# A tiny ScalarE write ahead of the second tile's load, in a two-tile row normalisation

## The chip, the cores and the metric

The kernel runs on one core of a Trainium2 chip. The metric is the device time of one execution in microseconds, lower is better. Executions of one kernel here agree within about 0.6% (81.74 to 82.21 us in 34 runs of the kernel before), so effects of 0.3% are read from means over several runs, with a 95% interval. A run counts as slow when it is over 1.5% above the fastest run of its kernel. All runs that carry the argument are fast; the one kernel for which that is not so is marked. The granted clock is 1.0 in every run.

## The reference

```
norm = sqrt(sum(x ** 2, axis=-1, keepdims=True) + eps)     # x: 1024 x 4096 float32
return x / norm
```

Each of 1024 rows is divided by its own norm. 16.78 MB come in and 16.78 MB go out.

## The kernel before

The 1024 rows are two tiles of 128 partitions x 4 rows of 4096. Each tile has its own buffer, one load and one store of 8.4 MB, so nothing waits for a buffer. SyncE issues all four transfers on one queue. ScalarE squares and sums rows 0 to 2, VectorE row 3; ScalarE takes the roots, VectorE the reciprocals and nearly all scaling. In this cut (left-out lines are `...`, the comments are added) `R` is 4 rows and `D` is 4096.

```python
# class RowGroups: square_act, square_dve, norm (ScalarE root, VectorE reciprocal), scale (VectorE)
def scale_by_both(self, r):
    cut = 7 * self.D // 8        # ScalarE scales [:cut], VectorE the rest
    ...
groups = []
for i in range(n_tiles):
    g = RowGroups(nc, io, stats, scratch, D, R, eps_t)
    load = nc.sync.dma_start(out=g.flat(), in_=x_t[i])
    if i == 0:
        first_load_to_front(nc, load.ins)     # ahead of the opening barrier
    groups.append(g)
for i, g in enumerate(groups):
    g.square_dve(R - 1)
    g.square_act(0)
    g.norm(0)
    g.scale(0)
    g.square_act(1)
    g.norm(1)
    g.norm(R - 1)
    g.scale(1)
    g.scale(R - 1)
    g.square_act(2)
    g.norm(2)
    if i < n_tiles - 1:
        g.scale_by_both(2)
    else:
        g.scale(2)
    store = nc.sync.dma_start(out=out_t[i], in_=g.flat())
...
```

The build orders the instructions of each engine itself, within their dependences. The order of the source is not always the order that runs: in the first tile of this kernel, the build takes the root of row 3 (`g.norm(R - 1)`) ahead of the square of row 1. This matters below.

## Time and profile before

| | before |
|---|---|
| median time of 3 runs | 81.92 us (81.88 to 81.94) |
| span of the profile | 80.1 us |
| DMA queue, share of 16 engines | 97.3% |
| VectorE, ScalarE busy | 33%, 37% |
| issues of load 1, load 2, store 1, store 2 | 0.00, 0.79, 38.83, 56.62 us |

How to read it: the DMA engines work almost without a break, so the compute engines matter only through the moments at which they let a transfer be issued. The lines are shown in the prediction.

### The profile page before, as it was taken

To read this page: it belongs to the slowest core of one execution; us is meant where nothing else is said; L and a number is where in the kernel's file an instruction comes from. 1 tells how busy PE (TensorE), PEld (TensorE's weight loads), DVE (VectorE), ACT (ScalarE), POOL (GpSimd) and SP (SyncE) were. 2 spreads that over 40 slices of the span, in tenths; PEclk is the share of its full clock that TensorE was granted. 3 is DMA by queue.
4 is the path that set the end of the run, shared out by engine and by line. 5 is a ranking of instruction groups with operands and counts; after the bars stand their busy time and mean duration, and the time that the engine had idled before them with its cause. 6 is when DMAs were issued, how large, how long until landed. Compare 5 with 4: busy or idle time off the path is not lost.

```text
span 80.1 us, 93 instructions
## 1 busy us (share of the span) xinstructions
DVE 26.7 (33%) x21; ACT 29.7 (37%) x23; POOL 0.2 (0%) x4
## 2 busy tenths in 40 slices
DVE  0000000000099599960039995999200000000000
ACT  6000000000099999989339999950000000000000
POOL 0000000000000000000000000000000000000000
DMA  9199996599993899993999993999993999993990
GB/s 491 65 491 524 524 524 295 229 524 524 524 524 164 360 524 524 524 491 164 393 524 524 524 458 164 425 524 524 524 425 164 458 524 524 524 425 131 491 524 0
DMA packets 576, 33.55 MB, mean 419 GB/s; under 512 B 64, under 2 KB 64, under 8 KB 64
## 3 DMA queue, kind: packets, MB, share of 16 engines
q1 hardware_dynamic: 576, 33.55, 97.3%
HBM read 16.78 MB, written 16.78 MB: 419 GB/s over the span
## 4 chain that ended last, share of the span: by engine, by line
DMA 50%; ACT 10%; DVE 9%; issue 0%
DMA xt<-in_x_dram 50%; ACT sq_act L33 9%; DVE xt L64 9%; ACT rstd L53 1%; DVE rstd L59 0%
## 5 line engine op out<-in xcount | busy, mean ns | idle before, releaser
L33 ACT ACTIVATE sq_act<-xt 128x4096 f32<-128x4096 f32 x6 | 21.7, 3608 | 22.3 <-DMA xt<-in_x_dram 22.3
L42 DVE SCALAR_TENSOR_TENSOR sq_dve<-xt 128x4096 f32<-128x4096 f32 x2 | 8.9, 4426 | 26.3 <-DMA xt<-in_x_dram 26.3
L64 DVE TENSOR_SCALAR xt<-xt,rstd 128x4096 f32<-128x4096 f32 x7 | 16.5, 2354 | 0.2
L72 ACT ACTIVATE xt<-xt,rstd 128x3584 f32<-128x3584 f32 x1 | 3.3, 3282 | 0.2 <-DVE rstd L59 0.2
L53 ACT ACTIVATE rstd<-ssq,eps_t 128x1 f32<-128x1 f32 x8 | 2.1, 288 | 0.1
L59 DVE RECIPROCAL rstd<-rstd 128x1 f32<-128x1 f32 x8 | 1.3, 160 | 2.4 <-ACT rstd L53 2.4
L33 ACT ACT_TABLE_LOAD x1 | 1.3, 1283 | 0.8 <-PEq L256 0.8
L53 ACT ACT_TABLE_LOAD x1 | 1.3, 1283 | 0.0
L33 ACT ACTIVATION_READ_ACCUMULATOR sq_act<-xt 128x1 f32 x6 | 1.1, 186 | 0.0
L78 DVE TENSOR_SCALAR xt<-xt,rstd 128x512 f32<-128x512 f32 x1 | 0.5, 486 | 0.0
L209 DVE MEMSET eps_t<- 128x1 f32 x1 | 0.1, 59 | 0.9 <-PEq L256 0.9
L42 DVE DVE_READ_ACCUMULATOR sq_dve<-xt 128x1 f32 x2 | 0.2, 83 | 0.0
L256 POOL MEMSET const-bfloat16-1.0<- 128x1 bf16 x1 | 0.1, 102 | 0.0
L256 POOL MEMSET const-uint8-127<- 128x1 uint8 x1 | 0.1, 101 | 0.0
L256 POOL MEMSET const-float32-0.0<- 128x1 f32 x1 | 0.1, 99 | 0.2 <-issue 0.2
L256 POOL MEMSET const-float32-1.0<- 128x1 f32 x1 | 0.1, 98 | 0.0
## 6 DMA issues: line engine op xcount, KB each, us to landing
xt<-in_x_dram SPq DMA_DIRECT2D x2, 31.2
out_dram<-xt SPq DMA_DIRECT2D x2, 22.5
```

The costliest lines, as they stand in the source:

```text
L33: self.nc.scalar.activation(out=sq_a, in_=self.x[:, r], func=ACT_F.Square, accum_out=self.ssq[:, r : r + 1],)
L42: self.nc.vector.scalar_tensor_tensor(out=sq_v, in0=self.x[:, r], scalar=1.0, in1=self.x[:, r], op0=ALU.mult, op1=ALU.mult, accum_out=self ...
L53: self.nc.scalar.activation(out=self.rstd[:, r : r + n], in_=self.ssq[:, r : r + n], func=ACT_F.Sqrt, bias=self.eps_t,)
L59: self.nc.vector.reciprocal(out=self.rstd[:, r : r + n], in_=self.rstd[:, r : r + n])
L64: self.nc.vector.tensor_scalar_mul(out=self.x[:, r], in0=self.x[:, r], scalar1=self.rstd[:, r : r + 1])
L72: self.nc.scalar.activation(out=self.x[:, r, :cut], in_=self.x[:, r, :cut], func=ACT_F.Copy, scale=rstd,)
L78: self.nc.vector.tensor_scalar_mul(out=self.x[:, r, cut:], in0=self.x[:, r, cut:], scalar1=rstd)
L209: nc.vector.memset(eps_t, eps)
L256: nc = _bacc.Bacc("TRN2", target_bir_lowering=False, num_devices=1)
```

## The change

The second tile's first column gets a tiny write by ScalarE, so the second load, which overwrites it, must wait for that write. The evident intent is to keep the second load out of the way while the first one starts.

```diff
         g = RowGroups(nc, io, stats, scratch, D, R, eps_t)
+        if i == 1:
+
+            nc.scalar.activation(out=g.x[:, 0, 0:1], in_=eps_t, func=ACT_F.Square)
         load = nc.sync.dma_start(out=g.flat(), in_=x_t[i])
```

## The prediction

> **What bounds the kernel now.** I began with the page's busy shares and its DMA row, then the DMA queue, then the timeline around each transfer, then narrow windows at the start, because the rest turned out to have no room.
>
> ```profile
> DVE 26.7 (33%) x21; ACT 29.7 (37%) x23; POOL 0.2 (0%) x4
> DMA  9199996599993899993999993999993999993990
> ...
> q1 hardware_dynamic: 576, 33.55, 97.3%
> HBM read 16.78 MB, written 16.78 MB: 419 GB/s over the span
> ```
>
> The compute engines are busy a third of the span; the 16 DMA engines are busy 97.3% of it. So the kernel is bound by moving 33.55 MB, and 2.7% of 80.1 us, 2.2 us, is all the time in which they are not. The dips in the DMA row are no idle time: the program has four transfers (two loads, two stores) of 128 rows of 64 KB, thus 512 large packets, 32 for each engine, and a packet seems to be counted where it starts, so a slice in which few start looks empty. Two windows settle the length of one:
>
> ```profile
> core 0: us, DVE busy (x) ACT busy (x) POOL busy (x), PEclk, DMA share, GB/s
> 0.00:1.00 1.00, 0.06 (x1) 0.21 (x1) 0.20 (x4) 1.00 0.00 0
> 1.00:1.25 0.25, 0.00 (x0) 0.25 (x1) 0.00 (x0) 1.00 5.64 1835
> 1.25:1.50 0.25, 0.00 (x0) 0.25 (x1) 0.00 (x0) 1.00 2.89 1049
> 1.50:1.75 0.25, 0.00 (x0) 0.25 (x1) 0.00 (x0) 1.00 1.39 524
> 1.75:2.00 0.25, 0.00 (x0) 0.25 (x1) 0.00 (x0) 1.00 1.29 524
> 2.00:2.25 0.25, 0.00 (x0) 0.07 (x1) 0.00 (x0) 1.00 0.64 262
> ...
> 3.90:4.75 0.85, 0.00 (x0) 0.00 (x0) 0.00 (x0) 1.00 2.85 1234
> ...
> 37.75:38.50 0.75, 0.00 (x0) 0.75 (x1) 0.00 (x0) 1.00 3.24 1398
> ```
>
> The last two columns are the DMA share and the rate; the rate times the window's length, over 65,536 bytes, counts the packets that start in it. In 3.90:4.75 that is 1234 x 0.85 us = 1.05 MB = 16 packets, one for each engine, and 2.85 x 0.85 x 16 / 16 = 2.42 us each. At that length 32 packets take 77.4 us. In the first rows 7, 4, 2, 2 and 1 packets start, so the sixteen engines do not begin together: the first starts just after 1.0 us, the last just after 2.0 us. The first seven take 5.64 x 0.25 x 16 / 7 = 3.22 us each, the next four 2.89, then about 2.8 and 2.6. After that all is regular. The end follows: last engine starts at 2.0, plus 77.4, gives 79.4; its slow first packet and the landing account for the rest of the 80.1 us span. **The only slack is the first two microseconds**: a wait of 1.0 us before any packet, a stagger of 1.0 us, and a first packet that is up to 0.8 us too long.
>
> Next, whether compute ever holds up the DMA:
>
> ```profile
> 0.00 1.12 SPq L217 DMA_DIRECT2D xt<-in_x_dram  x2
> ...
> 0.79 1.28 ACT L33 ACT_TABLE_LOAD   x1 [0.79 <-PEq L256]
> 0.86 0.06 DVE L209 MEMSET eps_t<- 128x1 f32 x1 [0.86 <-PEq L256]
> ...
> 38.83 0.35 SPq L238 DMA_DIRECT2D out_dram<-xt  x1
> 41.26 3.62 ACT L33 ACTIVATE sq_act<-xt 128x4096 f32<-128x4096 f32 x1 [2.45 <-DMA xt<-in_x_dram]
> ...
> 56.62 0.34 SPq L238 DMA_DIRECT2D out_dram<-xt  x1
> ```
>
> The first store is issued at 38.83, while the second load lands at about 41.2: it queues 2.4 us ahead of need. The second store is issued at 56.62. The first store, begun when the load was done, lasts a quarter of 77.4 us, 19.4 us, to about 60.6: 4 us ahead of need. Both exceed the 1.0 us that an issue needs before its first packet (seen at the start). So the queue never runs dry, and nothing that ScalarE or VectorE does shows in the end time. The chain of waits charges "DMA xt<-in_x_dram 50%" from 0.79 us, the issue of the second load; that is the time it stands behind the first one in the queue, and starting it later need not move its landing.
>
> **What the Trainium skill says.** "DMA: Bandwidth & Descriptors", section "Queues, rings and completion order": on each DMA engine descriptors are consumed in ring order. The trace agrees: both loads are on q1 and land about 19.3 us apart (21.94 and 41.26), so the second does not share the rate with the first. The same page, "Where 436 GB/s comes from", gives a ceiling of 435.2 GB/s for the ports. Here 16 x 65,536 B / 2.42 us = 433 GB/s, so between packets there is nothing to win. "Perfetto Trace Analysis", its part on the HWDGE DMA instruction, says that the profiled span of an issue covers the generation of descriptors and not the movement. The trace agrees: an issue shows about 0.35 us, yet no packet starts before 1.0 us. "ScalarE: Activation LUTs", section "What ACT_TABLE_LOAD costs", gives 1283 ns for the load and 280 ns + 0.833 ns per element for an ACTIVATE with a pointer bias; the rows here have 1283 ns and 288 ns for 128x1.
>
> **The change part by part.** It adds one ACTIVATE of 128x1 on ScalarE before the second load is issued, and as that write goes to the same tile, the load must wait for it. Nothing is removed.
> - Its own cost: about 0.29 us (from the 128x1 Sqrt row) on an engine that would sit idle until 21.94. On the path: 0. It reads eps_t, ready at 0.92, and uses Square, the function whose table is loaded first anyway, so I expect no third table load.
> - The wait: the table load ends at 0.79 + 1.28 = 2.07; plus 0.29 is 2.36. The second load is issued at about 2.4 instead of 0.79, 1.6 us later. Its first packet is needed when the first load's eight packets per engine are done, at about 20.9 us at the earliest. With 1.0 us from issue to first packet it is ready at 3.4, some 17 us early. Cost on the path: 0.
> - What moves: the generation of the second load's descriptors leaves the stretch in which the first load's packets begin. It now falls between 0.79 and, by the 1.0 to 2.0 us that the first load's own took to reach its engines, some 1.8 to 2.8 us. That covers the late half of the stagger and the long first packets. This must be the intent: let the first load start undisturbed. At most it is worth the stagger plus a bit: if all engines started near 1.0 with packets of 2.42 us, the end would come at 1.0 + 77.4 plus the same tail, 1.0 to 1.2 us earlier. But a transfer needs some time to reach sixteen engines whatever follows it, and a first packet also waits for its first bytes, so I give the second load less than half of it: 0.4 us. Against that stands the same disturbance at its new place, 2.4 to 4.4 us. The first store's issue at 38.83 shows its size in full flow: packets started in 37.75:38.50 last 3.24 x 0.75 x 16 / 16 = 2.43 us instead of 2.42, thus 0.01 us. Hence about -0.4 us in all: 81.92 to 81.5.
>
> **The rivals.**
> 1. No overlap matters: the stagger and the long first packets belong to the first load itself (cold memory, its own descriptors). For it: the earliest engines, started at 1.0 to 1.2, are the slow ones, which looks like a wait common to all that ends at about 2 us, rather than a queue behind the second load. Then the time is 81.9.
> 2. A real gain at the start, the whole stagger: 80.8 to 81.0. For it: the first load has the stretch to itself until 2.4. Against it: the second load's issue begins only 0.2 us before the first packets.
> 3. The wait moves trouble into the first packets, still running until 4.6 us: the descriptors arrive at 3.4 to 4.4, and if they slow packets as much as the start seems to, the gain is given back, or up to 0.3 us lost: 82.2. Against it: the 0.01 us at the first store.
> 4. The delay uncovers the second load, or a table is loaded thrice and the first store is late. The margins are 17 us and 2.4 - 1.0 = 1.4 us against 1.6 us and 1.28 us; the second margin is close, but the first tile's table reload at 25.7 exists already. I give this 1%.
>
> **Range and chances.** The limits are the slack at the start on one side, 1.2 us, and the small disturbance on the other. I predict 81.5 us and a range of 80.8 to 82.1. Two per cent is 1.64 us, more than the whole stagger and the long first packets together can give; only if the 1.0 us wait before the first packet also shrank would it be reached, and that wait begins before the second load is issued. So: faster by over 2% 0.02, within 2% 0.96, slower by over 2% 0.02.
>
> **What would show it.** In the trace after, one more 128x1 ACTIVATE at about 2.1 us, the second load's issue near 2.4, still two table loads, and both landings moved by the same small amount as the end. The windows from 1.0 to 2.25 should have more packets early and a mean nearer to 2.42 us; if their counts stay 7, 4, 2, 2, 1 with the same means, rival 1 holds. If the windows around 3.9 to 4.75 show packets well over 2.42 us, rival 3 does. The prediction is wrong in kind if the gap between the two landings exceeds 19.4 us, or if the issue of the first store comes after the second load has landed.

## The result, and the profile after

The kernel after takes 82.28 us (median of 6 runs, 82.2 to 82.43) against 81.93 us of the kernel before in the same session (6 runs). The ratio is 1.0041, 95% interval 1.0028 to 1.0054. Ratios here are the mean time of one kernel's fast runs over that of the other's of the same rounds, so not quite the ratio of the medians quoted. The change makes the kernel slower by 0.35 us. It is within 2%, as predicted (in part by luck, see below), but outside the range of 80.8 to 82.1, and in the opposite direction to the gain that was predicted.

The tiny write and the wait came out as worked out. From the timeline of the kernel after (start, duration, engine, line, operation):

```profile
0.79 1.28 ACT L219 ACT_TABLE_LOAD   x1 [0.79 <-PEq L259]
2.09 0.20 ACT L219 ACTIVATE xt<-eps_t 128x1 f32<-128x1 f32 x1
2.31 0.33 SPq L220 DMA_DIRECT2D xt<-in_x_dram  x1
```

The start did not get faster. These are the windows of the kernel after at the start; the last two columns are DMA share and GB/s, read as in the prediction:

```profile
1.00:1.25 0.25, 0.00 (x0) 0.25 (x1) 0.00 (x0) 1.00 7.16 2359
1.25:1.50 0.25, 0.00 (x0) 0.25 (x1) 0.00 (x0) 1.00 2.20 786
1.50:1.75 0.25, 0.00 (x0) 0.25 (x1) 0.00 (x0) 1.00 0.00 0
1.75:2.00 0.25, 0.00 (x0) 0.25 (x1) 0.00 (x0) 1.00 1.84 786
2.00:2.25 0.25, 0.00 (x0) 0.24 (x2) 0.00 (x0) 1.00 0.61 262
...
3.90:5.00 1.10, 0.00 (x0) 0.00 (x0) 0.00 (x0) 1.00 2.20 953
```

Now 9, 3, 0, 3 and 1 packets start, instead of 7, 4, 2, 2 and 1. Summed up, the sixteen first packets take 0.25 x 16 x (7.16 + 2.20 + 1.84 + 0.61) / 16 = 2.95 us on average; the same sum over the prediction's rows gives 2.96 us. The first load starts just as slowly with the second one out of the way. The second packets, in 3.90:5.00, last 2.20 x 1.10 x 16 / 16 = 2.42 us as before, so the wait did no harm there either (rival 3). Both loads also land as before (the second tile's work starts at 41.29 instead of 41.26).

The loss is at the border between the last load and the first store. First the kernel before, then the kernel after, same windows. The first row of each block has the starts of the load's last packets, the next two have what follows them, and the last is near the end of the program:

```profile
37.80:38.50 0.70, 0.00 (x0) 0.70 (x1) 0.00 (x0) 1.00 3.47 1498
...
40.24:40.52 0.28, 0.00 (x0) 0.00 (x0) 0.00 (x0) 1.00 2.71 1170
40.52:40.92 0.40, 0.00 (x0) 0.00 (x0) 0.00 (x0) 1.00 4.17 1802
...
77.12:77.48 0.36, 0.00 (x0) 0.00 (x0) 0.00 (x0) 1.00 0.00 0
```

```profile
37.80:38.50 0.70, 0.00 (x0) 0.70 (x1) 0.00 (x0) 1.00 3.46 1498
...
40.24:40.52 0.28, 0.00 (x0) 0.00 (x0) 0.00 (x0) 1.00 0.01 0
40.52:40.92 0.40, 0.00 (x0) 0.00 (x0) 0.00 (x0) 1.00 5.01 2130
...
77.12:77.48 0.36, 0.00 (x0) 0.00 (x0) 0.00 (x0) 1.00 4.21 1820
```

In both kernels all sixteen engines start their last load packet between 37.80 and 38.50. In the kernel before, 1170 GB/s x 0.28 us / 65,536 B = 5 engines go on to a store packet between 40.24 and 40.52. In the kernel after none does: the first store packet starts at 40.53. By the records of the single packets, an engine now idles 0.21 us on average here, against 0.002 us before. At the end, 10 engines start their last packet after 77.12 that had all started it by then in the kernel before.

The cause is one step earlier. This is VectorE and ScalarE on the first tile, before and after:

```profile
26.96 0.48 ACT L53 ACTIVATE rstd<-ssq,eps_t 128x1 f32<-128x1 f32 x2
27.29 0.16 DVE L59 RECIPROCAL rstd<-rstd 128x1 f32<-128x1 f32 x1 [0.92 <-ACT rstd L53]
27.35 3.60 ACT L33 ACTIVATE sq_act<-xt 128x4096 f32<-128x4096 f32 x1
...
35.33 0.17 DVE L59 RECIPROCAL rstd<-rstd 128x1 f32<-128x1 f32 x1 [0.56 <-ACT rstd L53]
```

```profile
26.98 0.29 ACT L53 ACTIVATE rstd<-ssq,eps_t 128x1 f32<-128x1 f32 x1
27.18 3.60 ACT L33 ACTIVATE sq_act<-xt 128x4096 f32<-128x4096 f32 x1
...
30.78 0.46 ACT L53 ACTIVATE rstd<-ssq,eps_t 128x1 f32<-128x1 f32 x2
31.09 0.16 DVE L59 RECIPROCAL rstd<-rstd 128x1 f32<-128x1 f32 x1 [1.23 <-ACT rstd L53]
...
36.02 0.15 DVE L59 RECIPROCAL rstd<-rstd 128x1 f32<-128x1 f32 x1
...
39.52 0.35 SPq L241 DMA_DIRECT2D out_dram<-xt  x1
```

Before, ScalarE takes two roots (rows 3 and 0) at 26.96, ahead of its next big square, so VectorE has two rows to scale while that square runs. After, it takes only the root of row 0, then squares row 1 for 3.6 us, and only then takes the roots of rows 3 and 1. VectorE idles 1.23 us up to 31.09, works the rest off in a row, and comes to the last reciprocal at 36.02 instead of 35.33. The first store is issued at 39.52 instead of 38.83, 0.69 us later. The diff says nothing of this order: the build chose it. The late order is the order of the source; the early one was the build's own doing, and with the added write it did not do so.

### The profile page after: what moved, and what is told of

Same layout as the page of the kernel before. It is cut to its first block, busy times and chain, and to the rows that moved or that the text cites. A ratio compares the mean times of both kernels' runs of the same rounds, so it can differ in the third digit from the quotient of the medians.

```text
span 80.5 us, 94 instructions
## 1 busy us (share of the span) xinstructions
DVE 26.7 (33%) x21; ACT 29.8 (37%) x24; POOL 0.2 (0%) x4
## 4 chain that ended last, share of the span: by engine, by line
DMA 48%; ACT 12%; DVE 9%; issue 0%
DMA xt<-in_x_dram 48%; ACT sq_act L33 9%; DVE xt L64 9%; ACT L219 2%; ACT rstd L53 1%; DVE rstd L59 0%; ACT xt L219 0%
```

## The experiments

Twelve experiments ran, on eleven kernels (the last is a second look at one); all gave correct results. The edits are shown shortened, with lines joined. The first four take the change apart.

**late_order.** The kernel before, with an ordering edge (a dependence given to the build) and nothing else; the arguments of the edge and two `return` lines are left out here:

```diff
+        sq1 = g.square_act(1)
         g.norm(1)
-        g.norm(R - 1)
+        root = g.norm(R - 1)
+        if i == 0:
+            # edge without semaphore: root after sq1 on ScalarE
```

> The kernel before, with nothing but ScalarE's order in the first tile forced to that of the kernel after (the square root of row 3 after the square of row 1). No tiny write, no wait. Theory A (the order makes the first store late): first store issued near 39.5 us, its first packets about 1.0 us later at 40.5 instead of 40.24, time 82.2 to 82.35. Theory B (the wait of the second load costs): unchanged, 81.9.

Measured: 82.26 us, ratio 1.0033 (1.0022 to 1.0045). The first store was issued at 39.49. Its windows:

```profile
40.18:40.41 0.23, 0.00 (x0) 0.00 (x0) 0.00 (x0) 1.00 0.01 0
40.41:40.86 0.45, 0.00 (x0) 0.00 (x0) 0.00 (x0) 1.00 4.79 2039
```

No store packet starts before 40.41, though the first engine's load packets were done at 40.19. The order alone, with no write and no wait, brings the whole loss.

**early_order.** The kernel after, with the opposite edge: in the first tile the root of row 3 is taken before the square of row 1. The tiny write and the wait stay.

> The kernel after with its tiny write and its wait, but ScalarE's order in the first tile forced back to that of the kernel before. Theory A: second load issued near 2.3 us, first store near 38.8 us, no gap before the store's packets, time 81.85 to 82.0. Theory B (the wait or the write costs by itself): stays at 82.2 to 82.35.

Measured: 81.93 us, ratio 0.9997 (0.9988 to 1.0006). Second load issued at 2.30, first store at 38.78. The same windows:

```profile
40.18:40.41 0.23, 0.00 (x0) 0.00 (x0) 0.00 (x0) 1.00 2.64 1140
40.41:40.86 0.45, 0.00 (x0) 0.00 (x0) 0.00 (x0) 1.00 4.04 1748
```

4 and 12 packets start, without a pause. So the tiny write and the wait together cost nothing and gain nothing that shows.

**op_alone.** The tiny write goes to a scratch column; the second load waits for nothing.

```diff
-            nc.scalar.activation(out=g.x[:, 0, 0:1], in_=eps_t, func=ACT_F.Square)
+            nc.scalar.activation(out=stats.tile([P, 1], F32, name="tiny"), in_=eps_t, func=ACT_F.Square)
```

> The tiny Square writes to a scratch column, so that the second load waits for nothing. The build gives ScalarE the order of the kernel after. Theory A: second load issued near 0.8 us again, first store still near 39.5 us, time 82.2 to 82.35. Theory B (the wait): 81.9. My theory at the prediction (the late second load helps the start a little): 82.5, as that help would be gone.

Measured: 82.27 us, ratio 1.0038 (1.0025 to 1.0051). Second load at 0.78, first store at 39.51. The mere presence of the instruction makes the build choose the later order. My reason at the prediction, that a late second load helps the start, missed: with the load early again nothing was lost.

**wait_dve.** The write is a memset on VectorE, so there is a wait but no ScalarE instruction (shown against the kernel after).

```diff
-            nc.scalar.activation(out=g.x[:, 0, 0:1], in_=eps_t, func=ACT_F.Square)
+            nc.vector.memset(g.x[:, 0, 0:1], 0.0)
```

> The tiny write is a memset on VectorE instead, so the second load waits, but only to about 1.0 us, and the build keeps ScalarE's order of the kernel before. Theory A: first store near 38.8 us, time 81.85 to 82.0. Theory B (any wait for a write): 82.1 or more.

Measured: 81.89 us, ratio 0.9998 (0.9988 to 1.0007); second load at 0.97, first store at 38.70, and the build kept the earlier order. These four leave one cause: the order. That it acts through the late store is tested next.

The next ones ask how late is too late, and what it costs.

**after_cut58.** The kernel after, `cut = 5 * self.D // 8` in place of `7 * self.D // 8`, so that ScalarE's share of the last scaling ends sooner.

> The kernel after as it is (tiny write, wait and ScalarE's late order), but the last scaling of the first tile cut at 5/8 instead of 7/8, so that ScalarE's part takes about 3.28 - 1024 x 0.833 ns = 2.43 us. Theory A (only the moment of the first store counts, it must be issued by 40.24 - 1.01 = 39.2 us): store issued near 38.7 us, no gap, time 81.85 to 82.0. If the order or the tiny write costs in any other way, it stays near 82.25.

Measured: 81.97 us, ratio 1.000 (0.999 to 1.001), first store at 38.63, no gap. Order, write and wait are those of the kernel after; a store 0.89 us earlier is enough to undo the loss. So the order costs only through the moment of the first store.

**before_cut63.** The kernel before with `cut = 63 * self.D // 64`.

> The kernel before with the last scaling of the first tile cut at 63/64, so that ScalarE's part takes 448 x 0.833 ns = 0.37 us longer. The first store should be issued near 39.2 us, at the limit. Theory A with its limit of 39.2: gap of 0.0 to 0.05 us, time 81.9 to 82.05. If any delay of the store costs from the start (a slope without a limit): 82.25 or so.

Measured: 82.09 us, ratio 1.002 (1.0012 to 1.0029), first store at 39.15. The time is just outside what I expected, as my limit of 39.2 was wrong. Call the time from the issue to the moment when an engine is done with the load that engine's lead. The engines were done from 40.16 to 40.84. By the records of the single packets, three of them, with leads of 1.45, 1.59 and 1.69 us, went straight on to a store packet of 2.42 us; the other thirteen, with leads of 1.01 to 1.51 us, idled 0.21 us on average (0.17 us over all sixteen). In the kernel before, issued at 38.83, the smallest lead was 1.41 us (first engine done at 40.24) and no engine idled; in the kernel after the largest was 1.40 us and all did. So a store's issue must come about 1.4 to 1.5 us before an engine runs out, not 1.0 us, and the limit is not a sharp one.

**late_cut63.** The forced late order plus the cut at 63/64.

> The forced late order on the kernel before, plus the cut at 63/64: first store near 39.86 us. Theory A: the gap grows by the same 0.37 us, from 0.2 to about 0.57 us, time 82.26 + 0.37 = 82.6 to 82.7. If the loss of late_order was a fixed price of missing the limit: 82.26 again.

Measured: 82.18 us, ratio 1.0033 (1.0021 to 1.0045), first store at 39.77. The expectation missed: 0.28 us more delay than in late_order, and the mean gap went only from 0.20 to 0.23 us. So it is not a gap that grows with the delay from the limit on; the price looks fixed.

**late_split.** As late_cut63, with ScalarE's last scaling in four pieces. This separates a fixed price from one that grows later.

```diff
-        self.nc.scalar.activation(out=self.x[:, r, :cut], in_=self.x[:, r, :cut], func=ACT_F.Copy, scale=rstd)
+        for a in range(0, cut, cut // 4):
+            self.nc.scalar.activation(out=self.x[:, r, a : a + cut // 4],
+                in_=self.x[:, r, a : a + cut // 4], func=ACT_F.Copy, scale=rstd)
```

> Late order, cut at 63/64, and ScalarE's last scaling of the first tile made in four pieces, for some 0.5 us more: first store near 40.3 us. Theory C (an engine pays a fixed 0.2 us when its next descriptors are late, and beyond that only waits until they are there, 0.86 us after the issue in late_cut63): first store packets at about 40.3 + 0.86 = 41.2 us, mean gap 0.6 to 0.9 us, time 82.6 to 82.9. Theory D (one fixed price however late): 82.2 to 82.3 again.

Measured: 82.72 us, ratio 1.0096 (1.0082 to 1.0111), first store at 40.52. Its windows:

```profile
40.90:41.36 0.46, 0.03 (x1) 0.03 (x1) 0.00 (x0) 1.00 0.00 0
41.36:41.52 0.16, 0.16 (x1) 0.16 (x1) 0.00 (x0) 1.00 15.36 6554
```

All sixteen engines start at once after 41.36, 0.84 us after the issue, with a mean gap of 0.78 us. This is what theory C had. So for this store there are two regimes. An engine for which the issue comes too late, by the limit of about 1.4 us, but still well ahead pays about 0.2 us; one with a lead of less than about 0.6 us is idle until 0.84 to 0.99 us after the issue (late_split; the least in late_cut63 is 0.86). What the engine does in the 0.2 us is not shown.

The last four test the other margin of the prediction, that of the second load, by making it wait for a row of big VectorE writes to its tile (shown against the kernel after):

```diff
-            nc.scalar.activation(out=g.x[:, 0, 0:1], in_=eps_t, func=ACT_F.Square)
+            nc.vector.memset(g.x[:, 0], 1.0)
+            for k in range(5):      # wait_edge: 6; wait_gap: 6 and half a row more
+                nc.vector.tensor_scalar_mul(out=g.x[:, (k + 1) % 2], in0=g.x[:, k % 2], scalar1=1.0)
```

**wait_long.**

> The second load waits for six big VectorE writes to its tile, five of them of 2.35 us, and is issued only at about 15 to 17 us, 13 us later than in the kernel after; ScalarE's order is that of the kernel before. Theory A (the load needs its descriptors only at about 20.9 us, so it may be issued as late as 19.9): no gap, first store near 38.8 us, time 81.85 to 82.05. Theory B (a late second load costs): clearly over 82.3.

Measured: 81.89 us, ratio 1.0002 (0.9993 to 1.001). The load was issued at 16.87 and cost nothing.

**wait_edge.**

> As wait_gap, but without the last half write: the second load is issued near 19.2 us, some 1.7 us before the first engine runs out of packets (20.9). In before_cut63 engines with a lead of 1.0 to 1.5 us ran dry and the one with 1.7 did not. Theory C: no gap between the loads, or at a few engines only, time 81.85 to 82.1. If the long row of VectorE writes beside the landing load was what cost 3 us in wait_gap: 84 or more here too.

Measured: 82.03 us, ratio 1.0004 (0.9993 to 1.0015), the load issued at 19.21, 1.79 us before the first engine's next packet at 21.00; no gap. Leads between 1.05 us (wait_gap) and 1.79 us were not tried for a load.

**wait_gap and wait_gap_again.** The load was issued at 20.46 and 20.47.

> The second load is issued at about 20.3 us, after the limit; ScalarE's order is that of the kernel before. Theory C: a gap of 0.2 to 0.4 us between the two loads, all later times moved by it, time 82.1 to 82.4; the first store, still near 38.8, leaves no gap. Should packets after this gap last 2.42 us and the stores 2.418 us, then the longer store packets (2.424 us) of the kernel after come with a store that starts late, not with any gap. If the wait for the write is free at any length: 81.9.

Measured: 85.37 us (84.11 to 85.59). Only three of its six runs count as fast (84.11, 84.64, 85.34); they give the ratio 1.034 (1.0293 to 1.0387). The profile fell in a run counted as slow, so the kernel was looked at once more:

> The same kernel as wait_gap, for a second profile: its six times ran from 84.1 to 85.6 and its profile fell in a run called slow. If the loss belongs to the second load's dry start, one or a few engines start or run their first packets late again, and the second load lands at 42 us on most engines and well after 43 on the last; the time is 84 to 85.6. If it was an accident of that profile, the landings lie within 0.7 us of each other as elsewhere.

Measured: 85.37 us, one run of unknown state. Its profile shows the same picture as the first one: the second load lands from 42.03 to 44.59 us (42.13 to 44.64 in wait_gap). Windows of wait_gap:

```profile
20.80:21.40 0.60, 0.00 (x0) 0.00 (x0) 0.00 (x0) 1.00 0.01 0
21.40:22.40 1.00, 0.52 (x1) 0.52 (x1) 0.00 (x0) 1.00 3.11 1049
```

No packet starts until 21.40, and the first packets of this load take 3.11 x 1.00 x 16 / 16 = 3.11 us on average, as long as at the start of the program. I had expected a gap of 0.2 to 0.4 us and no more; that missed by far. The engine that lands last adds it up, by the records of its packets: 0.80 us later start than the last engine of the kernel before (22.37 against 21.57), 1.12 us in a first packet of 3.54 us, and 1.52 us in a last packet of 3.94 us, 3.4 us in all. Why that last packet, after the first store had been queued behind it at 38.78, took so long is not explained. The longer store packets did not follow: after this gap the first store's packets took 2.418 us in both profiles. wait_edge, with nearly the same row of VectorE writes, shows that the writes beside the landing load are not what costs.

## Why the prediction was wrong

- **What bounds the kernel: right.** The DMA engines do, and packets of 2.42 us leave no room between them. The same reading found no room for a loss either, which was the mistake below.
- **The cost of the tiny write and of the wait: right.** 0.20 us on an idle engine (estimated 0.29), the load issued at 2.31 (estimated 2.4), no third table load, and early_order shows a sum of zero within its interval (0.9988 to 1.0006). The large margin of the second load was real: wait_edge could issue it at 19.21.
- **The gain at the start, "I give the second load less than half of it: 0.4 us": wrong, it is zero.** Rival 1 had the outcome right; its reasons (cold memory, the load's own descriptors) were not tested. First packets average 2.95 us with the second load away and 2.96 us with it (2.95 to 3.16 and 2.96 to 3.17 over all profiles), and a load that begins with idle engines at 21.4 us in wait_gap takes 3.11 us again. The slow start belongs to the load that starts.
- **"What moves: the generation of the second load's descriptors": the step that failed.** Something else moved too, ScalarE's order in the first tile. I read the diff as one added instruction in an otherwise fixed program; the build orders each engine anew. That put the first store's issue at 39.52 instead of 38.83, and each engine idled 0.21 us on average before it. Rival 4 named a late first store, gave it only a third table load as a reason, and 1%. The signs that the prediction set for being wrong in kind did not show this: the landings are still 19.3 us apart, and the store is issued 1.8 us before the second load has landed.
- **"It queues 2.4 us ahead of need", with a margin of "2.4 - 1.0 = 1.4 us": mis-sized.** The need was taken from the landing of the load at 41.2, when the last engine has landed. What counts is when the first engine runs out, 40.24. And the lead that an issue needs was taken as the 1.0 us from the program's start; before_cut63 puts it at 1.4 to 1.5. The true margin is about 0.3 us at most (38.83 is free, 39.15 is not), and 0.69 us of delay exceeds it. With the right margin, a late first store would not have been a 1% case.
- **"Within 2%": right, in part by luck.** The prediction had bounded the gain, by the slack at the start. It had no bound for a late store, which here cost 0.35 us; wait_gap shows that a transfer issued too late can cost over 2%.
- **The sum of the loss.** A round here is one packet on each of the 16 engines. From the packets' records of the two profiles, averaged over engines: 0.21 us of gap, 0.04 us in the first store packets (2.458 us instead of 2.418), 0.025 us in the round that ends the first store, and 0.077 us from the other fourteen rounds at about 2.424 us. The sum is 0.35 us, as measured. So only 0.21 us is the gap itself; 0.14 us are longer packets. The longer packets came in all six profiles whose first store started after a gap (after, late_order, op_alone, before_cut63, late_cut63, late_split), and in none of the six that had no gap anywhere. Why they stay longer to the end is open.
- **Why the build changes the order** when a ScalarE instruction comes first is not shown by these runs; only that it does (op_alone), and does not for the VectorE one (wait_dve). In the second tile both kernels run in the source's order.

None of the versions is faster than the kernel before by more than the noise.

## What to carry to other kernels

Where a build orders the instructions, compare each engine's order before and after a change, even of one instruction: here that was the whole effect. In a kernel bound by transfers, measure the slack of each issue against the moment when the first engine runs out, not when the last one lands, and keep an issue clear of that moment (here every lead of 1.54 us or more was free). If such a slack is small, make it larger (a cut of 5/8 did that here) before the next change eats it.

## What the Trainium skill lacked or had wrong

- "DMA: Bandwidth & Descriptors", section "Latency and other measured facts": gives about 600 ns to the first byte for transfers issued by SyncE. Here the first packet started 0.84 us (late_split) to 1.02 us (start of the program) after the issue.
- The same page, section "Rules for kernel authors", says to issue a transfer early but not how early behind another one. Here, on one queue, 1.41 us before the first engine ran out was free (before), and leads of 1.0 to 1.5 us (before_cut63) cost 13 of 16 engines about 0.2 us each.
- No page has that first packets of a load on idle engines take longer: 2.95 to 3.17 us on average for 64 KB, against 2.42 us in full flow, with or without a second transfer behind it. First packets of a store after a gap took 2.46 us.
- No page has that packets stay longer when the first store starts after a gap: 2.424 us instead of 2.418, for nearly 40 us.
